# S5 products in fixed alternating rows, weights staged by half units, and the weights behind PLE ordered after the parts of x

## The chip, the cores and the metric

The kernel runs on one core of one Trainium2 chip. The metric is the device time of one execution in microseconds (us), the median of several runs. Nothing runs beside it on the chip's other cores.

## The reference

Two decoder layers over 256 tokens of width 1024, in float32. Each layer is `LN(a*x + 0.5*SwiGLU_1(x))`, then `LN(a*x + Mix(x))`, then `LN(a*x + 0.5*SwiGLU_2(x))`, then the gated embedding (PLE) `x + sigmoid(x Wg) * (p Wp)`. SwiGLU has an inner width of 2816. The mixer of layer 0 joins a Mamba-2 SSD (16 heads) and an S5 (64 groups of 16 channels, 64 complex states each); the mixer of layer 1 joins HGRN2 and GLA.

The S5 part matters here. Per group, `bu = B_bar u`, a diagonal complex recurrence `s[l] = lam_bar * s[l-1] + bu[l]`, and `y = Re(C s) + d * u`, followed by GELU and a gated projection. The kernel works on blocks of four time steps, so that there are 64 blocks in the sequence of 256: one product (`W`) folds a block's inputs into the states, a scan over the blocks carries them, one product (`Q`) reads the state before each block out, and one product (`T`) holds what a block's own inputs add to its outputs.

## The kernel before

**Weights.** All large weights lie in one array of units of 128 x 2048 float32 (1 MB). `Weights.unit` (L45) loads the next unit into a staging tile `wst` (two buffers of a whole unit), then splits each half `j` of it: ScalarE writes the rounded half `wh` (L61), VectorE writes the rest `wl` (L62). Every product with weights is three TensorE products (`wh` with `xh`, `wl` with `xh`, `wh` with `xl`). The split tiles have six buffers each, three units. The load is issued by SyncE, whose queue waits until VectorE has read the buffer's former contents.

**Order.** The program is written once, in Python, and a scheduler puts the instructions of each engine into an order of its own, by a simulated time line; buffers go round in program order. Each engine then runs its list strictly in that order on the chip. Two helpers bind the scheduler: `late` keeps an instruction where the program has it, and `behind(g, ins, anchors)` (L90) puts an instruction after named earlier ones of its own engine, as an order and not as a wait. `Weights.behind[n]` holds such anchors for unit `n`. `layer_norm` sets them for the units `at+1` and `at+2` of the next stage (last line of L117 to L145), `at` being the next unit to be loaded; `ple` sets none.

**Stages.** FFN 0 of layer 0 (`f00`), with the S5 parameters computed between its steps by `s5_scalars`, `s5_half` and `s5_params`; mixer AB; FFN 2 (`f01`); `ple_proj` and `ple` of layer 0; the same for layer 1 with mixer CD. An FFN has 11 steps of 256 inner columns: two units for gate and up (tile `gu_f`), one for down (tile `acc_f`). Its first step is `tile_major`: both units are loaded, and the products of token tile 0 come ahead of those of tile 1.

**S5 parameters.** For each of 8 batches of 8 groups, `s5_params(b)` computes tables on VectorE and returns `rest`, called a step later: 16 products of 64 x 64 (tile `s5w`, L543) turn two parts `i` of `E` round into two tiles `tp[0]`, `tp[1]` of the `tr` ring (two buffers in PSUM), which ScalarE copies out.

**S5 recurrence.** `s5_batches` (L661) is called four times in `ab_inputs`, for two batches `e = 0, 1` each, with the other projections of the mixer between the calls. It loads `W`, `tab`, `T` and `Q`; forms `v` of both batches (32 products of 64 x 64, L684) in the two buffers of the `mm` ring; and then, batch after batch on VectorE: `rotate`, two scans, `rotate` again into `S`. Then `y` of both batches (48 products, L712 for `T` and L715 for `Q`) in the `mm` ring again, and ScalarE copies `y` into `G`. A product takes 64 rows of the array, `row_half(0)` or `row_half(1)`. The program text lets `e = 0` and `e = 1` alternate, always in different halves, but nothing holds the scheduler to that. In the trace each of these float32 products is two MATMUL instructions.

**PLE.** `ple` forms `acc` for two halves `c` of the columns and two token tiles `t`; `finish(t, c)` takes tanh, combines, transposes the new `x` (tile `tp_ple`, L311) and splits it into `xh_ple`, `xl_ple` with `split_xT` (L112, L113). `split_xT` leaves its two instructions in `g.anchors`.

Of the kernel before, what the change touches and what calls it, by code (L numbers as in the profile page):

```python
# [17 lines left out]
P = 128  # L18
# [19 lines left out]
class Weights:  # L38
# [6 lines left out]
    def unit(self, pool=None):  # L45
        g, nc = self.g, self.g.nc
        pool = pool or g.wsp
        n = self.at
        self.at += 1
        st = g.wst.tile([P, 2048], F32, tag="wst", name=f"wst_{n}")  # L50
        step = {0: 512, 1: 1024, 2: 1024}.get(n, 2048)
        for c in (slice(i, i + step) for i in range(0, 2048, step)):
            nc.sync.dma_start(st[:, c], self.wall[n][:, c])
        out = []
        for j in range(2):
            wh = pool.tile([P, 1024], F32R, tag="wh", name=f"wh_{n}_{j}")
            wl = pool.tile([P, 1024], F32R, tag="wl", name=f"wl_{n}_{j}")
            src = st[:, j * 1024:(j + 1) * 1024]
            step = 512 if n == 0 else 1024
            for c in (slice(i, i + step) for i in range(0, 1024, step)):  # L60
                ops = [nc.scalar.copy(wh[:, c], src[:, c])]  # L61
                ops.append(nc.vector.tensor_tensor(wl[:, c], src[:, c], f32(wh[:, c]), op=ALU.subtract))  # L62
                for op in ops:
                    behind(g, op, self.behind.get(n, ()))
            out.append((wh, wl))
        return out
# [213 lines left out]
def ple(g, i, pp, out):  # L280

    nc = g.nc
    xT_in = g.xT
    last = out is not None
    acc = acc_tiles(g, f"ple{i}")
    units = [[None, None], [None, None]]
    xT = None if last else new_xT(g, f"ple{i}")
    xn = g.x

    def part(t, c, kh):  # L290
        for j in range(4):
            k = 4 * kh + j
            wh, wl = units[c][kh][j // 2]
            s = slice(512 * (j % 2), 512 * (j % 2) + 512)
            mm3(nc, acc[t][c], *of_tile(xT_in, t, k), wh[:, s], wl[:, s], k == 0, k == KT - 1)

    def finish(t, c):
        step = 256 if last and t == NT - 1 and c else 512
        for s in (slice(i, i + step) for i in range(512 * c, 512 * c + 512, step)):
            a = acc[t][c][:, s.start - 512 * c:s.stop - 512 * c]  # L300
            sg = g.pp.tile([P, step], F32, bufs=2, tag="ple_sg", name=f"sg_ple{i}_{t}_{s.start}")
            nc.scalar.activation(sg, a, AF.Tanh, scale=0.5)
            nc.vector.scalar_tensor_tensor(sg, sg, 1.0, pp[t][:, s], op0=ALU.add, op1=ALU.mult)
            nc.vector.scalar_tensor_tensor(xn[t][:, s], sg, 0.5, xn[t][:, s], op0=ALU.mult, op1=ALU.add)
            if last:
                nc.sync.dma_start(out[t * P:(t + 1) * P, s], xn[t][:, s])
        if last:
            return
        tp = g.ps.tile([P, 4, P], F32, tag="tr", name=f"tp_ple{i}_{t}_{c}", bufs=2)
        for k in range(4):  # L310
            nc.tensor.transpose(tp[:, k, :], xn[t][:, (4 * c + k) * P:(4 * c + k + 1) * P], g.ident)  # L311
        split_xT(g, t, c, tp, xT)

    for kh in range(2):
        units[0][kh] = g.w.unit()
    for t in range(NT):
        for kh in range(2):
            part(t, 0, kh)
    for t in range(NT):
        finish(t, 0)  # L320
    for kh in range(2):
        units[1][kh] = g.w.unit()
    for t in range(NT):
        for kh in range(2):
            part(t, 1, kh)
        finish(t, 1)
    g.xT = xT
# [172 lines left out]
def s5_params(g, b, half):  # L500
# [34 lines left out]
    def rest():  # L535
        W, K = g.s5pe
        Ev, Qv = (x.rearrange("p a (q n) -> p a q n", q=NP) for x in (E, Q))
        tp = [g.ps.tile([P, NP, 64], F32, tag="tr", name=f"s5w_{b}_{i}", bufs=2) for i in range(2)]
        for turn in range(2):
            for q in range(NP):  # L540
                for i in range(2):
                    r = row_half(turn ^ i)
                    nc.tensor.matmul(tp[i][r, q, :], Ev[r, i, q, :], g.ident[r, r], start=True, stop=True)  # L543
        for i in range(2):
            nc.scalar.copy(W[:, i], tp[i])
        kp = g.ps.tile([P, 64], F32, tag="tr", name=f"s5k_{b}", bufs=2)
# [87 lines left out]
    return ap.rearrange("p k (s c) -> p k s c", s=4)  # L634


def s5_inputs(g, pool, U, c):

    nc = g.nc
# [18 lines left out]
        nc.gpsimd.dma_start(to, dv[:, :, :, st, :])  # L658


def s5_batches(g, pool, U, G, bs):  # L661

    nc = g.nc
    mul, add, sub = ALU.mult, ALU.add, ALU.subtract
    W, T, Q, tab, S = [], [], [], [], []
    for b in bs:
        dram = g.s5dram[b]
        W.append(pool.tile([P, 2, NP, 64], F32, tag="W", name=f"W_{b}", bufs=3))  # L670
# [5 lines left out]
        Q.append(pool.tile([P, 2, NP, 80], F32, tag="Q", name=f"Q_{b}", bufs=3))  # L676
        nc.scalar.dma_start(Q[-1], dram[:, 1280:1920].rearrange("p (a q c) -> p a q c", a=2, q=NP))
    v = [g.ps.tile([P, 2, NP, 64], F32, tag="mm", name=f"s5v_{b}", bufs=2) for b in bs]
    for turn in range(2):
        for i in range(2):  # L680
            for q in range(NP):
                for e, b in enumerate(bs):
                    r = row_half(turn ^ e)
                    nc.tensor.matmul(v[e][r, i, q, :], W[e][r, i, q, :], U[r, NP * b + q, :], start=True, stop=True)  # L684

    for e, b in enumerate(bs):
        cosT, sinT, dec = (tab[e][:, 256 * i:256 * i + 256] for i in range(3))
        w = pool.tile([P, 2, 256], F32, tag="rw", name=f"rw_{b}", bufs=1)

        def rotate(src, name, out, ops):  # L690

            c = pool.tile([P, 2, 256], F32, tag="rotc", name=f"{name}c_{b}", bufs=2)
            s = pool.tile([P, 2, 256], F32, tag="rots", name=f"{name}s_{b}", bufs=2)
            nc.vector.tensor_tensor(c, src, bc(cosT, 1, 2), op=mul)
            nc.vector.tensor_tensor(s, src, bc(sinT, 1, 2), op=mul)
            for i in range(2):
                nc.vector.tensor_tensor(out[:, i], c[:, i], s[:, 1 - i], op=ops[i])

        m = pool.tile([P, 2, 256], F32, tag="rotm", name=f"rotm_{b}", bufs=1)
        rotate(v[e].rearrange("p a q c -> p a (q c)"), "rot", m, (add, sub))  # L700
        for i in range(2):
            nc.vector.tensor_tensor_scan(w[:, i], dec, m[:, i], 0.0, op0=mul, op1=add)
        S.append(pool.tile([P, 2, NP, 64], F32, tag="S", name=f"S_{b}", bufs=2))
        rotate(w, "rov", S[-1].rearrange("p a q c -> p a (q c)"), (sub, add))
    y = [g.ps.tile([P, NP, 64], F32, tag="mm", name=f"s5y_{b}", bufs=2) for b in bs]
    for turn in range(2):
        for q in range(NP):
            for i in range(-1, 2):
                for e, b in enumerate(bs):
                    r = row_half(turn ^ e)  # L710
                    if i < 0:
                        nc.tensor.matmul(y[e][r, q, :], T[e][r, q, :], U[r, NP * b + q, :], start=True,  # L712
                                         stop=False)
                    else:
                        nc.tensor.matmul(y[e][r, q, 1:64], Q[e][r, i, q, 16:80], S[e][r, i, q, 0:63],  # L715
                                         start=False, stop=i == 1)
    for e, b in enumerate(bs):
        lo = NP * b % 16
        nc.scalar.copy(G[:, lo:lo + NP, :], y[e])
# [252 lines left out]
def ab_inputs(g, pool, s5pool, yh, yl):  # L972
# [36 lines left out]
    U = s5pool.tile([P, 32, 64], F32, tag="U", name="U", bufs=1)  # L1009
    for c in range(2):  # L1010
        s5_inputs(g, pool, U, c)
    yT = []

    def recur(n):
        if n % 2 == 0:
            half.append(pool.tile([P, 16, 64], F32, tag="G", name=f"G_{n // 2}", bufs=1))
        s5_batches(g, s5pool, U, half[-1], (2 * n, 2 * n + 1))
        if n == 1:
            yT.append(s5_half_out(g, half[-1], 0, yh, yl))

# [278 lines left out]
def tile_trunk(ctx: ExitStack, tc: tile.TileContext, xnat, xTd, pT, lnr, colsd, cstd, abrow, abdt, s5bc, cdlr, cdgu,  # L1299
# [3 lines left out]
    g.nc, g.tc = nc, tc  # L1303
    g.abrow, g.abdt, g.s5bc, g.cdlr, g.cdgu = abrow, abdt, s5bc, cdlr, cdgu
    g.const = ctx.enter_context(tc.tile_pool(name="const", bufs=1))
    g.wst = ctx.enter_context(tc.tile_pool(name="wst", bufs=2))
    g.wsp = ctx.enter_context(tc.tile_pool(name="wsp", bufs=6))
    g.xp = ctx.enter_context(tc.tile_pool(name="xp", bufs=1))
    g.xt = ctx.enter_context(tc.tile_pool(name="xt", bufs=1))
# [225 lines left out]
```

## Time and profile before

| | |
|---|---|
| time, median of 3 runs | 1238.76 us (1238.2 to 1241.11) |
| the profiled execution | 1242.7 us, of which the span from the first to the last instruction is 1240.9 us |
| TensorE (PE) busy | 1210.4 us, 98% |
| weight loads into the array (PEld) | 1005.9 us, 81% |
| VectorE (DVE) busy | 854.5 us, 69% |
| ScalarE (ACT) busy | 583.9 us, 47% |
| GpSimd (POOL) busy | 72.4 us, 6% |
| DMA | 232.74 MB, 188 GB/s in the mean |
| granted TensorE clock | 0.993 in the mean |

Busy time is a union of modelled spans: matmuls are pipelined, so that a busy PE is not one at its peak, and successive starts tell what an instruction costs in a run. The profiled execution lies 3.9 us above the median of the three runs; the prediction works with differences from it.

### The profile page before, as it was taken

The numbers are of one execution on the slowest core, as the hardware profiler recorded it, in microseconds if no ns is written. First come the engines' busy times: TensorE is split into PE (matmuls) and PEld (weight loads), VectorE is DVE, ScalarE is ACT, GpSimd is POOL, SyncE is SP. The second block draws the span as 40 slices with busy tenths as digits, with TensorE's granted clock in tenths as the row PEclk, the third lists the DMA queues.
The fourth block names the chain that finished last, engine by engine and source line by source line (L and its number), as shares of the span: only waits on it lengthen the run. The fifth ranks groups of instructions, "written<-read, shape, count | busy, mean of one in ns | idle before, by whom it ended". The sixth has DMA issues, their size and how long they took to land.

```text
span 1240.9 us, 17250 instructions
## 1 busy us (share of the span) xinstructions
PE 1210.4 (98%) x6786; PEld 1005.9 (81%) x6786; DVE 854.5 (69%) x1352; ACT 583.9 (47%) x866; POOL 72.4 (6%) x124
## 2 busy tenths in 40 slices
PE   7999999999998999999998999999999999999998
PEld 6877777899887878888887888888888877888886
DVE  6999894688878766555567555456779776545466
ACT  5644452545535535443435444443674625444434
POOL 0012122110203000000000000000100010000000
PEclk9999999899999999999999999999999999999999
DMA  7567676775722647555536555554633327555532
GB/s 282 203 233 251 230 243 229 267 250 175 219 95 66 220 146 252 179 198 179 195 136 203 204 190 184 198 177 168 224 135 107 133 77 247 194 186 187 192 147 102
DMA packets 44609, 232.74 MB, mean 188 GB/s; under 512 B 9680, under 2 KB 10352, under 8 KB 20848
## 3 DMA queue, kind: packets, MB, share of 16 engines
q1 hardware_dynamic: 30672, 206.06, 48.2%
q0 software_dynamic: 4688, 14.16, 3.6%
q10 hardware_dynamic: 9168, 11.42, 2.8%
q8 instruction: 53, 0.87, 0.3%
q14 instruction: 28, 0.23, 0.1%
HBM read 219.56 MB, written 12.06 MB: 187 GB/s over the span
## 4 chain that ended last, share of the span: by engine, by line
PE 90%; DVE 4%; DMA 3%; ACT 2%; issue 1%; ACTq 0%; SPq 0%; DVEq 0%
PE gu_f L178 38%; PE acc_f L72 7%; PE acc_f L71 6%; PE acc_f L70 6%; DMA wst<-in_wall_dram 2%; PE pj_z L178 2%; PE ht_f L215 2%; DVE wl L62 2%; PE s5y L715 1%; PE acc_ab L72 1%; PE acc_ab L71 1%; PE acc_ab L70 1%; PE pj_u L178 1%; PE s5w L543 1%; PE pj_hg L178 1%; PE pj_gr L178 1%
## 5 line engine op out<-in xcount | busy, mean ns | idle before, releaser
L62 DVE TENSOR_TENSOR wl<-wst,wh 128x1024 fp32r<-128x1024 f32 (+1 forms) x378 | 453.1, 1216 | 259.3 <-ACT wh L61 251.5
L61 ACT CAST wh<-wst 128x1024 fp32r<-128x1024 f32 (+1 forms) x378 | 386.9, 1047 | 359.4 <-PE gu_f L178 109.0
L71 PE MATMUL acc_f<-wl,hh_f 128*128 128x512 f32 x352 | 137.9, 392 | 0.0
L70 PE MATMUL acc_f<-wh,hh_f 128*128 128x512 f32 x352 | 137.5, 390 | 0.0
L72 PE MATMUL acc_f<-wh,hl_f 128*128 128x512 f32 x352 | 135.9, 392 | 0.0
L72 PEld LDWEIGHTS acc_f<-wh,hl_f 128*128 128x128 f32 x352 | 66.1, 188 | 13.8
L71 PEld LDWEIGHTS acc_f<-wl,hh_f 128*128 128x128 f32 x352 | 66.1, 188 | 13.6
L70 PEld LDWEIGHTS acc_f<-wh,hh_f 128*128 128x128 f32 x352 | 66.1, 188 | 13.6
L178 PE MATMUL gu_f<-wh,xh_in 128*128 128x512 f32 x176 | 71.1, 409 | 5.9 <-ACT wh L61 5.9
L178 PE MATMUL gu_f<-wh,xh_ple 128*128 128x512 f32 x176 | 70.9, 403 | 3.5 <-ACT xh_ple L112 3.5
L178 PE MATMUL gu_f<-wh,xh_ab 128*128 128x512 f32 x176 | 69.8, 397 | 0.5 <-ACT xh_ab L112 0.5
L178 PE MATMUL gu_f<-wl,xh_ab 128*128 128x512 f32 x176 | 68.8, 391 | 1.3 <-DVE wl L62 1.3
L178 PE MATMUL gu_f<-wh,xh_cd 128*128 128x512 f32 x176 | 69.9, 397 | 0.0
L178 PE MATMUL gu_f<-wl,xh_in 128*128 128x512 f32 x176 | 69.8, 400 | 0.0
L178 PE MATMUL gu_f<-wl,xh_cd 128*128 128x512 f32 x176 | 68.8, 391 | 0.7 <-DVE wl L62 0.7
L178 PE MATMUL gu_f<-wl,xh_ple 128*128 128x512 f32 x176 | 69.5, 395 | 0.0
L211 ACT ACTIVATE sg_f<-gu_f 128x256 f32<-128x256 f32 x88 | 33.8, 384 | 70.4 <-PE gu_f L178 69.1
L178 PE MATMUL gu_f<-wh,xl_ab 128*128 128x512 f32 x176 | 66.9, 391 | 0.0
L178 PE MATMUL gu_f<-wh,xl_cd 128*128 128x512 f32 x176 | 66.8, 391 | 0.0
L178 PE MATMUL gu_f<-wh,xl_ple 128*128 128x512 f32 x176 | 66.7, 391 | 0.0
L178 PE MATMUL gu_f<-wh,xl_in 128*128 128x512 f32 x176 | 66.6, 392 | 0.0
L212 DVE TENSOR_TENSOR sg_f<-sg_f,gu_f 128x256 f32<-128x256 f32 x88 | 36.7, 417 | 27.2 <-ACT sg_f L211 27.0
(466 smaller groups left out, 2387.2 us busy)
## 6 DMA issues: line engine op xcount, KB each, us to landing
wst<-in_wall_dram SPq DMA_DIRECT2D x185, 1024.0 KB, 4.8
row<-in_lnr_dram SPq DMA_DIRECT2D x12, 512.0 KB, 6.7
s5d<-s5pk POOLq DMA_DIRECT2D x8, 704.0 KB, 5.1
tab<-s5d ACTq DMA_DIRECT2D x8, 384.0 KB, 3.5
Q<-s5d ACTq DMA_DIRECT2D x8, 320.0 KB, 4.2
wst<-in_wall_dram SPq DMA_DIRECT2D x4, 512.0 KB, 6.6
s5d<-s5W POOLq DMA_DIRECT2D x8, 256.0 KB, 4.6
W<-s5d ACTq DMA_DIRECT2D x8, 256.0 KB, 3.7
```

The source lines that it names most:

```text
L61: ops = [nc.scalar.copy(wh[:, c], src[:, c])]
L62: ops.append(nc.vector.tensor_tensor(wl[:, c], src[:, c], f32(wh[:, c]), op=ALU.subtract))
L70: nc.tensor.matmul(out, xh, wh, start=first, stop=False)
L71: nc.tensor.matmul(out, xh, wl, start=False, stop=False)
L72: nc.tensor.matmul(out, xl, wh, start=False, stop=last)
L178: nc.tensor.matmul(ps[t], x, w, start=kh == 0 and i == 0, stop=kh == 1 and i == len(mms) - 1)
L211: nc.scalar.activation(sg, ps[t][:, 0:256], AF.Silu)
L212: nc.vector.tensor_tensor(sg, sg, ps[t][:, 256:512], op=ALU.mult)
L215: nc.tensor.transpose(tp[:, k, :], sg[:, k * P:(k + 1) * P], g.ident)
L543: nc.tensor.matmul(tp[i][r, q, :], Ev[r, i, q, :], g.ident[r, r], start=True, stop=True)
L715: nc.tensor.matmul(y[e][r, q, 1:64], Q[e][r, i, q, 16:80], S[e][r, i, q, 0:63], start=False, stop=i == 1)
```

## The change

- `Weights.unit` stages half units: a tile of 128 x 1024, four buffers instead of two of twice the size; each half has a load of its own (512 KB, one instruction; four of 256 KB in all for unit 0, as before; units 1 and 2 were already loaded in two pieces). The splits are the same.
- `ple`: after the split of the second column half of tile `t`, `behind[at + 1 + t]` is set to the anchors, so that both engines' splits of the second unit behind PLE come after those of tile 0's second half, and those of the third unit after tile 1's.
- `in_row` puts each S5 product after the one before it on TensorE. In `rest` the 16 products keep the written order, alternating between row halves. In `s5_batches` both `v` and `y` keep a fixed order in which `e = 1` and `e = 0` alternate.
- In `y` the two `Q` products come first and `T` last, so that a group of products begins with one that needs `S` of batch 1. `S` holds the states shifted by one block, with a column of zeros put there once by GpSimd, so that `Q` products are 64 columns wide instead of 63; the last `rotate` writes 63 of 64 columns.

```diff
@@ Weights.unit
-        st = g.wst.tile([P, 2048], F32, tag="wst", name=f"wst_{n}")
-        step = {0: 512, 1: 1024, 2: 1024}.get(n, 2048)
-        for c in (slice(i, i + step) for i in range(0, 2048, step)):
-            nc.sync.dma_start(st[:, c], self.wall[n][:, c])
         out = []
         for j in range(2):
+            st = g.wst.tile([P, 1024], F32, tag="wst", name=f"wst_{n}_{j}")
...
             for c in (slice(i, i + step) for i in range(0, 1024, step)):
-                ops = [nc.scalar.copy(wh[:, c], src[:, c])]
-                ops.append(nc.vector.tensor_tensor(wl[:, c], src[:, c], f32(wh[:, c]), op=ALU.subtract))
+                nc.sync.dma_start(st[:, c], self.wall[n][:, 1024 * j + c.start:1024 * j + c.stop])
+            for c in (slice(i, i + step) for i in range(0, 1024, step)):
+                ops = [nc.scalar.copy(wh[:, c], st[:, c])]
+                ops.append(nc.vector.tensor_tensor(wl[:, c], st[:, c], f32(wh[:, c]), op=ALU.subtract))
@@ ple, finish
         split_xT(g, t, c, tp, xT)
+        if c:
+            g.w.behind[g.w.at + 1 + t] = g.anchors
@@ s5_params, rest
+        g.row = ()
         for turn in range(2):
             for q in range(NP):
                 for i in range(2):
                     r = row_half(turn ^ i)
-                    nc.tensor.matmul(tp[i][r, q, :], Ev[r, i, q, :], g.ident[r, r], start=True, stop=True)
+                    in_row(g, nc.tensor.matmul(tp[i][r, q, :], Ev[r, i, q, :], g.ident[r, r], start=True, stop=True))
@@ new
+def in_row(g, op):
+    behind(g, op, g.row)
+    g.row = (op.ins,)
@@ s5_batches, v
-                for e, b in enumerate(bs):
+                for e in (1, 0):
                     r = row_half(turn ^ e)
-                    nc.tensor.matmul(v[e][r, i, q, :], W[e][r, i, q, :], U[r, NP * b + q, :], start=True, stop=True)
+                    in_row(g, nc.tensor.matmul(v[e][r, i, q, :], W[e][r, i, q, :], U[r, NP * bs[e] + q, :], start=True,
+                                               stop=True))
@@ s5_batches, S and y
-        S.append(pool.tile([P, 2, NP, 64], F32, tag="S", name=f"S_{b}", bufs=2))
-        rotate(w, "rov", S[-1].rearrange("p a q c -> p a (q c)"), (sub, add))
+        rotate(w, "rov", S[e][:, :, :, 1:64], (sub, add), 63)
...
-            for i in range(-1, 2):
-                for e, b in enumerate(bs):
+            for i in range(3):
+                for e in (1, 0):
                     r = row_half(turn ^ e)
...
+                    k, x = (Q[e][r, i, q, 16:80], S[e][r, i, q, :]) if i < 2 else (T[e][r, q, :], U[r, NP * bs[e] + q, :])
+                    in_row(g, nc.tensor.matmul(y[e][r, q, :], k, x, start=i == 0, stop=i == 2))
@@ ab_inputs
+    S = [s5pool.tile([P, 2, NP, 64], F32, tag=f"S{e}", name=f"S{e}", bufs=1) for e in range(2)]
+    for e in range(2):
+        nc.gpsimd.memset(S[e][:, :, :, 0:1], 0.0)
@@ tile_trunk
-    g.wst = ctx.enter_context(tc.tile_pool(name="wst", bufs=2))
+    g.wst = ctx.enter_context(tc.tile_pool(name="wst", bufs=4))
```

## Rows read from the trace of the kernel before

**Rows 1.** The page, part 1: busy time, share, instructions by engine.
```profile
PE 1210.4 (98%) x6786; PEld 1005.9 (81%) x6786; DVE 854.5 (69%) x1352; ACT 583.9 (47%) x866; POOL 72.4 (6%) x124
```
**Rows 2.** The page, part 4: the chain that ended last, by engine.
```profile
PE 90%; DVE 4%; DMA 3%; ACT 2%; issue 1%; ACTq 0%; SPq 0%; DVEq 0%
```
**Rows 3.** Waits of PE, 250 to 368 us: total us, times, longest.
```profile
PE xs L996 <- ACT xsT L813: 0.2, 1, 0.2
```
**Rows 4.** Windows: start:end, length, busy by engine, PEclk, DMA share, GB/s.
```profile
20.00:216.00 196.00, 195.48 (x1173) 156.58 (x1172) 166.63 (x333) 95.43 (x161) 27.68 (x58) 1.00 0.66 231
...
250.00:360.00 110.00, 109.79 (x1108) 100.07 (x1107) 95.78 (x182) 52.19 (x71) 9.59 (x16) 1.00 0.63 197
360.00:400.00 40.00, 34.95 (x243) 28.02 (x241) 30.88 (x74) 19.48 (x44) 8.39 (x14) 0.96 0.17 41
```
**Rows 5.** Windows of tile `s5v` alone (PE, PEld, DVE): first two calls, sum.
```profile
250.00:262.00 12.00, 2.08 (x64) 1.94 (x64) 1.28 (x2) 1.00 0.85 263
...
280.00:300.00 20.00, 3.74 (x64) 3.52 (x64) 2.57 (x4) 1.00 0.56 177
...
sum 120.00, PE 14.14 PEld 12.79 DVE 10.27; mean PE 1.77 PEld 1.60 DVE 1.28
```
**Rows 6.** Windows of tile `s5y` alone (PE, PEld, DVE, ACT): one batch, sum.
```profile
300.00:310.00 10.00, 2.71 (x46) 2.58 (x46) 0.00 (x0) 0.38 (x1) 1.00 0.51 154
...
sum 120.00, PE 25.02 PEld 22.40 DVE 0.00 ACT 2.99; mean PE 3.13 PEld 2.80 DVE 0.00 ACT 0.37
```
**Rows 7.** Windows of tile `s5w` alone (PE, PEld, ACT): two stretches, sum.
```profile
60.00:75.00 15.00, 1.15 (x32) 1.01 (x32) 0.64 (x2) 1.00 0.59 210
...
115.00:130.00 15.00, 0.96 (x16) 0.82 (x16) 0.98 (x3) 1.00 0.81 265
...
sum 145.00, PE 14.44 PEld 12.25 ACT 5.53; mean PE 1.44 PEld 1.23 ACT 0.55
```
**Rows 8.** Timeline of PE: one `T` product among full-size products (start, us).
```profile
262.37 0.28 PE L581 MATMUL pc_bc<-xh_f,wl 128*128 128x256 f32 x1
262.57 0.32 PE L712 MATMUL s5y<-U,T 64*64 64x64 f32 x2
262.83 0.39 PE L579 MATMUL pc_bc<-xh_f,wh 128*128 128x256 f32 x1
```
**Rows 9.** Timeline, ends of first and fourth call: `S` of batch 1, then users.
```profile
276.80 0.75 DVE L697 TENSOR_TENSOR S<-rovc,rovs 128x256 f32<-128x256 f32 x2
...
281.25 0.32 PE L715 MATMUL s5y<-S,Q 64*64 64x63 f32 x2
...
359.71 0.76 DVE L697 TENSOR_TENSOR S<-rovc,rovs 128x256 f32<-128x256 f32 x2
...
367.02 1.43 DVE L853 TENSOR_TENSOR xd<-xs,dt 128x256 f32<-128x256 f32 x4 [2.08 <-PE s5y L715]
```
**Rows 10.** Timeline behind PLE, ACT then PE; in brackets the idle time before.
```profile
678.46 1.05 ACT L61 CAST wh<-wst 128x1024 fp32r<-128x1024 f32 x1 [3.13 <-DMA wst<-in_wall_dram]
679.42 1.06 ACT L112 CAST xh_ple<-tp_ple 128x512 fp32r<-128x512 f32 x2
...
672.80 1.03 PE L311 MATMUL tp_ple<-cs,x_ln 128*128 128x128 f32 x8
...
680.05 0.80 PE L178 MATMUL gu_f<-wh,xh_ple 128*128 128x512 f32 x1 [3.47 <-ACT xh_ple L112]
...
683.20 0.49 PE L178 MATMUL gu_f<-wl,xh_ple 128*128 128x512 f32 x1
```
**Rows 11.** Window behind PLE, columns as in group 4.
```profile
680.00:690.00 10.00, 9.95 (x41) 8.13 (x42) 6.54 (x9) 4.99 (x7) 0.00 (x0) 0.83 0.70 245
```
**Rows 12.** Windows at start-up and in a later FFN; DMA issues (count, KB, us).
```profile
10.00:20.00 10.00, 10.00 (x42) 7.92 (x41) 6.76 (x10) 5.01 (x6) 0.00 (x0) 1.00 0.97 371
...
720.00:850.00 130.00, 130.00 (x590) 107.56 (x589) 69.13 (x81) 59.31 (x80) 0.00 (x0) 1.00 0.56 194
...
wst<-in_wall_dram SPq DMA_DIRECT2D x4, 512.0 KB, 6.6
```

More of the change, by code (lines that the diff above doesn't have):

```diff
@@ L49, in unit @@
         self.at += 1
-        st = g.wst.tile([P, 2048], F32, tag="wst", name=f"wst_{n}")
-        step = {0: 512, 1: 1024, 2: 1024}.get(n, 2048)
-        for c in (slice(i, i + step) for i in range(0, 2048, step)):
-            nc.sync.dma_start(st[:, c], self.wall[n][:, c])
         out = []
         for j in range(2):
+            st = g.wst.tile([P, 1024], F32, tag="wst", name=f"wst_{n}_{j}")
             wh = pool.tile([P, 1024], F32R, tag="wh", name=f"wh_{n}_{j}")
             wl = pool.tile([P, 1024], F32R, tag="wl", name=f"wl_{n}_{j}")
-            src = st[:, j * 1024:(j + 1) * 1024]
             step = 512 if n == 0 else 1024
             for c in (slice(i, i + step) for i in range(0, 1024, step)):
-                ops = [nc.scalar.copy(wh[:, c], src[:, c])]
-                ops.append(nc.vector.tensor_tensor(wl[:, c], src[:, c], f32(wh[:, c]), op=ALU.subtract))
+                nc.sync.dma_start(st[:, c], self.wall[n][:, 1024 * j + c.start:1024 * j + c.stop])
+            for c in (slice(i, i + step) for i in range(0, 1024, step)):
+                ops = [nc.scalar.copy(wh[:, c], st[:, c])]
+                ops.append(nc.vector.tensor_tensor(wl[:, c], st[:, c], f32(wh[:, c]), op=ALU.subtract))
                 for op in ops:
@@ L658, in s5_inputs, with s5_batches @@
         nc.gpsimd.dma_start(to, dv[:, :, :, st, :])
-def s5_batches(g, pool, U, G, bs):
+def s5_batches(g, pool, U, G, S, bs):
     nc = g.nc
     mul, add, sub = ALU.mult, ALU.add, ALU.subtract
-    W, T, Q, tab, S = [], [], [], [], []
+    W, T, Q, tab = [], [], [], []
     for b in bs:
@@ L678, in s5_batches @@
     v = [g.ps.tile([P, 2, NP, 64], F32, tag="mm", name=f"s5v_{b}", bufs=2) for b in bs]
+    g.row = ()
     for turn in range(2):
@@ L688, in s5_batches, with rotate @@
         w = pool.tile([P, 2, 256], F32, tag="rw", name=f"rw_{b}", bufs=1)
-        def rotate(src, name, out, ops):
+        def rotate(src, name, out, ops, n=64):
             c = pool.tile([P, 2, 256], F32, tag="rotc", name=f"{name}c_{b}", bufs=2)
@@ L696, in rotate @@
             for i in range(2):
-                nc.vector.tensor_tensor(out[:, i], c[:, i], s[:, 1 - i], op=ops[i])
+                parts = (x.rearrange("p (q c) -> p q c", q=NP)[:, :, 0:n] for x in (c[:, i], s[:, 1 - i]))
+                nc.vector.tensor_tensor(out[:, i], *parts, op=ops[i])
         m = pool.tile([P, 2, 256], F32, tag="rotm", name=f"rotm_{b}", bufs=1)
-        rotate(v[e].rearrange("p a q c -> p a (q c)"), "rot", m, (add, sub))
+        rotate(v[e].rearrange("p a q c -> p a (q c)"), "rot", m.rearrange("p a (q c) -> p a q c", q=NP), (add, sub))
         for i in range(2):
             nc.vector.tensor_tensor_scan(w[:, i], dec, m[:, i], 0.0, op0=mul, op1=add)
-        S.append(pool.tile([P, 2, NP, 64], F32, tag="S", name=f"S_{b}", bufs=2))
-        rotate(w, "rov", S[-1].rearrange("p a q c -> p a (q c)"), (sub, add))
+        rotate(w, "rov", S[e][:, :, :, 1:64], (sub, add), 63)
     y = [g.ps.tile([P, NP, 64], F32, tag="mm", name=f"s5y_{b}", bufs=2) for b in bs]
+    g.row = ()
     for turn in range(2):
         for q in range(NP):
-            for i in range(-1, 2):
-                for e, b in enumerate(bs):
+            for i in range(3):
+                for e in (1, 0):
                     r = row_half(turn ^ e)
[L711 to L716, printed above, removed]
+                    k, x = (Q[e][r, i, q, 16:80], S[e][r, i, q, :]) if i < 2 else (T[e][r, q, :], U[r, NP * bs[e] + q, :])
+                    in_row(g, nc.tensor.matmul(y[e][r, q, :], k, x, start=i == 0, stop=i == 2))
     for e, b in enumerate(bs):
@@ L1016, in recur @@
             half.append(pool.tile([P, 16, 64], F32, tag="G", name=f"G_{n // 2}", bufs=1))
-        s5_batches(g, s5pool, U, half[-1], (2 * n, 2 * n + 1))
+        s5_batches(g, s5pool, U, half[-1], S, (2 * n, 2 * n + 1))
         if n == 1:
```

## The prediction

> **What bounds the kernel.** I read the page's busy times first. PE is busy 98% of the span and VectorE 69% [rows 1]; the chain that ended last is PE for 90% [rows 2]. A busy PE is not yet a full one, so the next view is the list of PE's waits: behind PLE PE waits 3.5 us [rows 10], and in the 118 us in which the S5 recurrence runs PE waits 0.2 us [rows 3]. So in those stretches PE runs its list without a gap, and time goes only where the list gets shorter, or until another engine is the bound. The windows say which engine that would be [rows 4]. In FFN 0, where the S5 parameters are made, VectorE is busy 166.6 of 196 us (85%). Where the recurrence runs, it is busy 95.8 of 110 us (87%), and behind it, from 360 to 400 us, 30.9 of 40 us while PE has gaps. In a later FFN it is busy 69.1 of 130 us [rows 12]. VectorE is therefore the next bound in the mixer, and nowhere else where the change shortens PE's list.
>
> **Part 1, S5 products in the mixer.** The first call's `v` ran as the program text alternates it: 64 instructions in 2.08 us, 32.5 ns each. The second call's 64 took 3.74 us, 58 ns each; all four calls took 14.14 us [rows 5]. One batch's `y` took 2.71 us for 46 instructions, 59 ns each, and all of `y` 25.02 us for 384 instructions [rows 6]. The reader is to see two speeds of one instruction. I read the slow one as products that follow one another in the same row half: the scheduler ran one batch by itself as soon as it was ready. After the change every product's neighbour is in the other half and in the other batch's PSUM tile, as in the fast call.
> PE's list shortens by: `v` 14.14 - 4 x 2.08 = 5.8 us; `y` 25.02 - 384 x 0.0325 = 25.02 - 12.5 = 12.5 us. Together 18.3 us. Lone `T` and `Q` products that the scheduler scattered between full-size ones go too: around one of them the next full-size product starts 0.46 us after the last instead of 0.12 [rows 8], but most of that is in the tile's own 25.02 us, and I add nothing.
>
> The two speeds above are two ways through the array. The Trainium skill, "TensorEngine Tiling (Array Packing)", sections "Tiling Modes" and "Gotcha 1", says that different tiles of the array load and multiply in parallel, that changing the mode drains the array, and that two row tiles must not meet in one PSUM bank. By that `y` would gain as `v` does, up to twofold, so 25.02 would fall to about 12.5, the same as by the rows.
>
> How much of the 18.3 us ends up in the time is VectorE's to say. Its recurrence work is not shortened. Upper bound: all 18.3 us. Lower bound: VectorE keeps its 87% share, and only the end of the fourth call gains. There `S` of batch 1 is ready at 359.71 + 0.76 = 360.5 us and the SSD heads, whose buffers lie where S5's lay, start at 367.0 us behind the last `y` [rows 9]. With both `y` in one run of 96 x 0.0325 = 3.1 us plus the 0.3 us to the heads, 6.5 us become 3.4: 3.1 us gained. I take a VectorE share of 93%, between 87% and full, since both batches' `y` and then both new `v` now lie between the end of one call's VectorE work and the next one's, and other splits and convolutions can only partly fill it: 95.8 / 0.93 = 103.0 instead of 110, so 7.0 us. With the 3.1 us at the end: 10 us (3 to 18).
>
> The fixed order has a price of its own: PE stands at the first `y` until batch 1 is through VectorE. In the trace the first lone product of batch 1 was reached 281.25 - 277.56 = 3.7 us after `S` was ready [rows 9], so this margin covers it. Work queued behind that product on PE would wait: the projections, and ScalarE and VectorE behind them.
> The zero column, the wider `Q` products (64 for 63) and the 63-column writes cost nothing that I can see: `T` products of 64 columns run in the same 59 ns train as those of 63 [rows 6].
>
> **Part 2, S5 products in the parameters.** `s5w` took 14.44 us for 256 instructions. Where 32 came as one alternating run it took 1.15 us, where 16 came alone 0.96 us [rows 7]. Eight alternating runs are 8 x 1.15 = 9.2 us: 5.2 us less. The run starts only when both `tr` buffers are free, so the first half runs some us later than now; `s5k` and the FFN's transposes come behind it in that ring, with a step of the FFN, 196 / 11 = 17.8 us, as cover. Bounds 0 and 5.2; PE has no wait in this stage and VectorE is at 85% [rows 4], so I take a value near the upper end: 4 us.
>
> **Part 3, the weights behind PLE.** PE stood 3.47 us before the first product of the next FFN. It waited for `xh_ple`; the transposes for it had started at 672.80 us, but ScalarE's list had a weight split ahead of it, and that waited 3.13 us for its load to land at 678.4 us [rows 10]. That split belongs to the second unit, which the change puts behind the parts of `x`. With it out of the way `xh_ple` of the first half can be ready before PE is done with `acc`, and the stall goes. The first seven starts after it are 3.15 us / 7 = 0.45 us apart [rows 10], against 130 / 590 = 0.22 in a later FFN [rows 12], and the granted clock of 680 to 690 us is 0.83 [rows 11]: after the idle time PE ran at the lower of its two levels, 1.2 instead of 2.4 GHz. Without the idle time 7 x 0.22 = 1.5 us go as well. Together 5.0 us at most. What is late next is the second unit: its splits come about 4 us earlier at PE's need and now behind `x` of tile 0, whose tanh, two VectorE steps and transpose lie in between. If they come late, PE waits there instead. Bounds: 5 us gained and 2 us lost (one more split of 1.05 us on ScalarE and its VectorE partner ahead of PE); I take 4.5 us gained, since the load had landed at 678.4 us, and PE would want it at about 682 us: it would begin at 680.05 - 3.47 = 676.6 us and has 24 products of the first unit to do, 5.4 us.
>
> **Part 4, half units.** The splits are as before; 185 loads of 1 MB become 370 of half the size, on a queue that issues nothing else of weight. A half buffer is free one VectorE split (about 1.2 us) sooner, so loads start earlier. Cover: in a later FFN the units need 194 GB/s at a DMA share of 0.56 [rows 12], which is 346 GB/s at a full share. At the start of the kernel, where loads came in pieces of 512 KB and less, DMA moved 371 GB/s at 0.97 [rows 12]; smaller pieces therefore don't lower the rate that can be had. I take 0, with 3 us either way, since the scheduler's lists will come out otherwise in every stage.
>
> The 512 KB loads of the start took 6.6 us to land [rows 12]; four in flight at that latency are 4 x 0.524 MB / 6.6 us = 318 GB/s, over the 194 needed. Against this stands a rule of the Trainium skill, "DMA: Bandwidth & Descriptors", section "Bandwidth": move at least 1 MiB per transfer for three quarters of the peak. Its fit, 2 us plus bytes over 436 GB/s, would give 3.2 us and, as an estimate, 164 GB/s for one half unit at a time, which is under the rate needed; with several in flight, as the rows show, it binds nothing.
>
> **Sum.** 10 + 4 + 4.5 + 0 = 18.5 us. The profiled execution's 1242.7 us become 1224.2. It lies 3.9 us above the median of the runs, so the median becomes 1238.8 - 18.5 = 1220 us.
>
> **Rivals.**
> R1, PE's whole saving is kept: 18.3 + 5.2 + 5.0 = 28.5 us, 1210 us. For it: no wait of PE in these stages. Against: 110 us less 15 would leave VectorE's 95.8 us no gap at all.
> R2, VectorE is the bound at once: 3.1 us at the end of the recurrence, 1 us of the parameters, 4.5 us behind PLE, together 8 to 9 us, 1230 us. For it: 87% is a mean, and its work comes in chains that PE feeds.
> R3, no gain: the scheduler puts the fixed runs where PE waits for them, and the waits eat the saving, within 3.7 us of 1238.8 us.
> R4, slower, by one mechanism: PE parks at `y`. Today batch 0's `y` is done while VectorE works on batch 1. If PE's list reaches the fixed run ahead of `S` of batch 1, all that stands behind it stops. A batch takes VectorE some 10 us, so up to 9 us per call, 36 us in all, less 18.3 + 8.5: 9 us slower, 1248 us. It decides from (18.3 + 8.5) / 4 = 6.7 us of parking per call. Against it: the lag of 3.7 us in today's list must be used up first [rows 9].
> The skill's rule on transfer size, if it held with several loads in flight, would be a fifth: 164 of 194 GB/s in the FFN stages. Four loads at 318 GB/s speak against it, and I give it 1%, with R4.
>
> **How the numbers follow.** Forecast (11 to 25 us faster) 0.55; R1 0.09; R2 (4 to 11 faster) 0.20; R3 0.08; R4 and the rule 0.08. About 0.3%, 3.7 us, is what a measurement tells from no change. Faster 0.84, same 0.08, slower 0.08. The range 1210 to 1237 us holds the forecast, R2, half of R1 and part of R3, some 0.82. The likeliest case's own range is 1214 to 1228.
>
> **What would show it.** Right: `s5v`, `s5y` and `s5w` at about 8, 13 and 9 us of PE; VectorE above 90% in the recurrence; no wait for `xh_ple` and no low clock behind PLE; FFN steps of unchanged length. Wrong: a PE wait on `S` at L715's successor, PE waits for `wl` in FFN 0 or behind PLE, FFN steps longer by a DMA wait, or 58 ns per product though they alternate.

## The result: 1252.6 us, 1.07% slower

The kernel after the change takes 1252.55 us (median; 1248.63 to 1255.9), the kernel before 1238.7 us beside it: a ratio of 1.0107, 95% interval 1.0074 to 1.0139. 1220 us were predicted, 1210 to 1237 as the range. The sign was wrong.

The page of the kernel after, busy times (against [rows 1]) and the chain that ended last (against [rows 2]):

```profile
PE 1196.2 (96%) x6786; PEld 991.9 (79%) x6786; DVE 857.8 (69%) x1352; ACT 585.5 (47%) x865; POOL 72.8 (6%) x126
...
PE 76%; DVE 5%; DMA 5%; issue 4%; ACT 2%; POOL 0%; ACTq 0%; SPq 0%; DVEq 0%; POOLq 0%
```

PE does less work than before (1196.2 against 1210.4 us) in a span of 1251.3 us instead of 1240.9. So its list did get cheaper and the time went into gaps: PE's share of the chain fell from 90% to 76%.

Windows of the kernel after on the S5 tiles alone: `s5v`, `s5y`, `s5w` (against [rows 5 to 7]):

```profile
250.00:400.00 150.00, 10.17 (x256) 9.52 (x256) 10.26 (x16) 0.91 0.56 165
```
```profile
250.00:400.00 150.00, 16.95 (x384) 16.36 (x384) 0.00 (x0) 2.56 (x8) 0.91 0.56 165
```
```profile
60.00:220.00 160.00, 11.41 (x256) 9.36 (x256) 5.13 (x16) 0.99 0.67 229
```

The products gained 4.0, 8.1 and 3.0 us. What they gained is less than what PE lost waiting. PE's waits in the kernel after (total us, times, longest); the first two lines lie in the recurrence, where [rows 3] has 0.2 us in all, the last two in FFN 0, where the kernel before waits for neither `hh_f` nor `s5K`:

```profile
PE s5y L722 <- issue: 17.2, 2, 10.4
...
PE s5v L692 <- DMA U<-udram: 2.7, 1, 2.7
...
PE acc_f L68 <- ACT hh_f L216: 2.1, 4, 0.7
...
PE ht_f L213 <- ACT s5K L554: 1.6, 1, 1.6
```

Windows of the kernel after (PE, PEld, DVE, ACT, POOL, then granted clock, DMA share, GB/s); the first is FFN 0, the second the recurrence from the first `v` to the last `y` (against [rows 4]), the next two its second half, the last a `y` run behind a wait:

```profile
20.00:204.00 184.00, 180.63 (x1067) 142.72 (x1066) 158.60 (x316) 90.02 (x150) 22.47 (x48) 0.99 0.70 236
266.00:382.00 116.00, 96.68 (x1123) 90.38 (x1123) 91.29 (x177) 47.22 (x65) 9.60 (x16) 0.88 0.56 169
...
340.00:360.00 20.00, 9.59 (x141) 8.58 (x137) 17.05 (x30) 6.22 (x8) 5.69 (x11) 0.70 0.78 211
360.00:380.00 20.00, 13.19 (x202) 12.69 (x200) 10.28 (x20) 0.65 (x2) 0.00 (x0) 0.76 0.09 25
...
356.00:361.00 5.00, 5.00 (x95) 4.90 (x92) 1.29 (x2) 1.14 (x2) 0.00 (x0) 0.50 0.50 169
```

The third and fourth calls of the recurrence, timeline of PE in the kernel after:

```profile
339.10 2.08 PE L692 MATMUL s5v<-U,W 64*64 64x64 f32 x64
...
344.83 0.39 PE L176 MATMUL pj_z<-wh,xl_f 128*128 128x512 f32 x1
...
355.63 0.76 PE L722 MATMUL s5y<-S,Q 64*64 64x64 f32 x8 [10.41 <-issue]
...
363.97 2.08 PE L692 MATMUL s5v<-U,W 64*64 64x64 f32 x64
...
376.29 0.77 PE L722 MATMUL s5y<-S,Q 64*64 64x64 f32 x8 [6.81 <-issue]
```

and VectorE in the same stretch:

```profile
342.64 0.68 DVE L703 TENSOR_TENSOR rotc<-s5v,tab 128x512 f32<-128x512 f32 x1
...
355.11 0.75 DVE L707 TENSOR_TENSOR S<-rovc,rovs 128x252 f32<-128x252 f32 x2
...
366.11 0.69 DVE L703 TENSOR_TENSOR rotc<-s5v,tab 128x512 f32<-128x512 f32 x1 [6.51 <-PE s5v L692]
...
375.77 0.75 DVE L707 TENSOR_TENSOR S<-rovc,rovs 128x252 f32<-128x252 f32 x2
...
381.83 1.43 DVE L859 TENSOR_TENSOR xd<-xs,dt 128x256 f32<-128x256 f32 x4 [5.31 <-PE s5y L722]
```

Read the two together. PE reaches the tied `y` at 345.2 us and stands until VectorE writes `S` of batch 1, from 355.11 us on; then VectorE stands until the tied `v` is through, then PE again, then VectorE again. Each engine waits for the other in turn. After either wait PE runs at the lower of its two clock levels, 1.2 GHz: from 356 to 361 us the granted clock is 0.50 (in the two longer windows it is 0.70 and 0.76 in the mean), and the 96 instructions of `y` that take 3.0 us in the first call (290.88 to 293.89 us) take 5.5 us here (355.63 to 361.09 us). In the kernel before, `xd` came at 367.02 us [rows 9]: 14.8 us later now, of which 9.6 us had been lost before the first `v` (256.5 to 266.2 us), in FFN 0 and behind it, and 5.2 us within the recurrence. So there are two losses to explain, and the larger one lies ahead of the recurrence.

### The profile page after: what moved, and what is told of

It is laid out like the page before. It is cut to its first block, busy times and chain, and to the rows that moved or that the text cites. A ratio compares the mean times of both kernels' runs of the same rounds, so it can differ in the third digit from the quotient of the medians.

```text
span 1251.3 us, 17862 instructions
## 1 busy us (share of the span) xinstructions
PE 1196.2 (96%) x6786; PEld 991.9 (79%) x6786; DVE 857.8 (69%) x1352; ACT 585.5 (47%) x865; POOL 72.8 (6%) x126
## 4 chain that ended last, share of the span: by engine, by line
PE 76%; DVE 5%; DMA 5%; issue 4%; ACT 2%; POOL 0%; ACTq 0%; SPq 0%; DVEq 0%; POOLq 0%
PE gu_f L176 30%; PE acc_f L68 6%; PE acc_f L70 6%; PE acc_f L69 6%; DMA wst<-in_wall_dram 3%; PE pj_z L176 2%; PE ht_f L213 1%; PE acc_ple L69 1%; PE acc_ab L70 1%; PE acc_ab L68 1%; PE acc_ab L69 1%; PE acc_ple L68 1%; PE acc_ple L70 1%; DVE wl L60 1%; PE s5y L722 1%
## 5 line engine op out<-in xcount | busy, mean ns | idle before, releaser
L68 PEld LDWEIGHTS acc_f<-wh,hh_f 128*128 128x128 f32 x352 | 66.0, 188 | 17.3 <-ACT hh_f L216 4.0
L69 PEld LDWEIGHTS acc_f<-wl,hh_f 128*128 128x128 f32 x352 | 66.0, 188 | 13.6
## 6 DMA issues: line engine op xcount, KB each, us to landing
s5d<-s5W POOLq DMA_DIRECT2D x8, 256.0 KB, 4.7
W<-s5d ACTq DMA_DIRECT2D x8, 256.0 KB, 3.8
wst<-in_wall_dram SPq DMA_DIRECT2D x4, 256.0 KB, 5.9
```

What stands on the lines that cost most here:

```text
L68: nc.tensor.matmul(out, xh, wh, start=first, stop=False)
L69: nc.tensor.matmul(out, xh, wl, start=False, stop=False)
```

## The experiments

Theory at the outset: the loss is PE parked at `y`. Rivals: the half units' loads, and the fixed `s5w` in FFN 0. As the parts came in, two theories stood against each other: A, the cost comes from *tying* two PSUM tiles into one run, so that the run, and all that follows from it, waits for the later one; B, any fixed run costs, because it holds up what stands behind it. All ratios are to the kernel before on the same chip, with their 95% intervals.

**The parts alone, or together.** Each is the kernel before with these hunks of the diff and no others:

```
e1   Weights.unit and the wst pool (half units)
e2   ple: g.w.behind[g.w.at + 1 + t] = g.anchors
e5   in_row, rest                    (s5w)
e6   in_row, v                       (s5v)
e7   in_row, y, shifted S            (s5y)
e3   e5 + e6 + e7     e4   all but e7      e8   all but e5      e12  e1 + e5
```

> Only the staging in half units. Two theories for the 14 us lost: parking (PE stands 17 us at the fixed y runs, and that is all of it) and staging (FFN 0 and the start of mixer AB became 10 us longer, with waits for half-unit loads). Parking: no change beyond 4 us, 1235 to 1242 us. Staging: 1245 us or more, with the first v product of the S5 recurrence near 266 us instead of 256.5.

Measured: 1239.38 us, 1.0015 (0.9993 to 1.0037). No effect that can be told from none, as part 4's term of 0 had it.

> Only the order of the weights behind PLE. Both theories: the wait for xh_ple and the low clock behind it go, 4 to 5 us faster, 1234 us; no change elsewhere.

Measured: 1240.14 us, 1.0011 (0.9995 to 1.0027). No gain; both theories had expected one, and missed.

> Only the S5 products in fixed rows, all three kinds. Parking: 5 to 12 us slower, 1244 to 1251 us, with PE waits of 10 us or more at a y run. Staging: faster by 5 to 10 us, 1229 to 1234 us, without such waits, since nothing then delays the recurrence.

Measured: 1247.93 us, 1.0084 (1.0053 to 1.0115), with one wait of 9.6 us at `y`. The S5 runs alone are slower.

> The whole change but for y, which stays in the free order of before, T first. Parking: the waits go, and s5w, v and PLE keep their gains: 1225 to 1233 us. Staging: the 10 us of FFN 0 and the start of the mixer stay, 1240 us or more.

Measured: 1253.46 us, 1.0126 (1.0101 to 1.0151). This felled the theory at the outset: without the fixed `y` the kernel is as slow as with it. Parking at `y` is not the cause, or not the only one.

> Only the s5w products of FFN 0 in a fixed alternating order; staging, PLE and the mixer as before. Theory A (the fixed order makes FFN 0 longer, since the run needs both tr buffers and s5k and the transposes of the FFN stand behind it): s5w near 11 us of PE, the last gu_f of FFN 0 at 198 to 204 us instead of 195.8, PE waits for hh_f or s5K of 2 us or more, and 1241 to 1247 us. Theory B (FFN 0 is not the cause, the mixer is): last gu_f within 1.5 us of 195.8 and 1236 to 1240 us.

Measured: 1241.65 us, 1.0020 (1.0004 to 1.0035); last `gu_f` of FFN 0 at 200.3 us.

> Only the s5v products in a fixed alternating order; the list of PE is that of before up to the first s5v. Theory A (FFN 0 carries the loss): s5v from 14.1 to 8 to 10 us, first s5v at 256.5 us as before, 1234 to 1239 us. Theory B (a fixed run in the mixer is held up: it waits for both mm buffers and for W and U of both batches, and what stands behind it on PE waits with it): waits of PE before s5v of 2 us or more, last s5v later than 348.8 us by 3 to 10 us, 1241 to 1248 us.

Measured: 1245.27 us, 1.0057 (1.0041 to 1.0073), although `s5v` fell from 14.1 to 9.5 us; `s5y`, which was left free, rose from 25.0 to 29.1 us. PE does not wait at `v`, as theory B had it, but 5.2 us at the `y` behind it. This is the dearest of the five parts, and the one the prediction had not suspected. Timeline of PE in e6, first the products of the third call's `v`, then the last of `y` of the second call's batch 1:

```profile
309.79 0.32 PE L691 MATMUL s5v<-U,W 64*64 64x64 f32 x2
320.43 0.91 PE L691 MATMUL s5v<-U,W 64*64 64x64 f32 x22
```
```profile
316.80 0.39 PE L723 MATMUL s5y<-S,Q 64*64 64x63 f32 x4
```

and ScalarE and VectorE in e6:

```profile
317.42 0.37 ACT L727 COPY G<-s5y 128x256 f32<-128x256 f32 x1 [2.18 <-PE s5y L723]
```
```profile
323.22 1.23 DVE L62 TENSOR_TENSOR wl<-wst,wh 128x1024 fp32r<-128x1024 f32 x1 [6.34 <-ACT wh L61]
...
325.81 0.68 DVE L702 TENSOR_TENSOR rotc<-s5v,tab 128x512 f32<-128x512 f32 x1
```

The run is seen torn in two, in PE's list itself, since PE has other work in between: one product (two MATMUL instructions) goes into the free `mm` buffer at 309.79 us; the next one wants the other buffer, which holds `y` of batch 1 until the copy at 317.42 us; the rest of the run comes at 320.43 us. A buffer that could have fed VectorE lies open and unused for 10.6 us, and VectorE stands idle for 6.3 us before it has work again. In the kernel before, `v` of one batch went in from 311.54 us on, among the products of the other buffer's `y`.

> Only the s5y products in a fixed alternating order, with the shifted S; v, s5w, staging and PLE as before. Theory A (FFN 0 carries the loss): s5y from 25.0 to 13 to 17 us, waits of PE before s5y under 4 us in all, 1230 to 1239 us. Theory B (PE stands at the first product of a fixed y until S of the second batch is ready): waits before s5y of 8 us or more in all, calls three and four above all, y then at the lower clock, 1242 to 1250 us.

Measured: 1239.6 us, 1.0010 (0.9992 to 1.0027). PE waited 12.5 us in all at `y`, longest 6.8, and the time is that of before: here the wait and the saving cancel. That is the wait of theory B, with a time between the ranges of A and B.

> The whole change without the fixed order of s5w in FFN 0. Theory A: the loss of the whole change is mostly that of FFN 0, so last gu_f near 196 us, first s5v near 257 us, and 1236 to 1242 us. Theory B: FFN 0 as before, but PE still stands at s5y for 12 to 17 us in all, and 1246 to 1252 us.

Measured: 1248.37 us, 1.0086 (1.0067 to 1.0105); first `v` at 259.2 us, waits at `y` 10.6 us. So with `s5w` free most of the loss is still there; the next run shows that FFN 0 can lose as much without the mixer. The five parts alone add up to 0.15 + 0.11 + 0.20 + 0.57 + 0.10 = 1.13%, the whole measured 1.07%; that the two agree is chance, since not all the parts add.

> Half-unit staging and the fixed s5w rows together, mixer and PLE as before. Alone they moved the start of S5 by +1.2 and +3.2 us, in the whole change it is +9.6 us. Theory A (the two hurt each other in FFN 0): last gu_f of FFN 0 at 201 to 204 us, first s5v at 264 to 267 us, 1245 to 1249 us. Theory B (they only add, the rest comes from the other parts): last gu_f at 199 to 201 us, first s5v near 261 us, 1241 to 1244 us.

Measured: 1248.73 us, 1.0082 (1.0051 to 1.0113); last `gu_f` at 202.6 us, first `v` at 264.4 us. These two parts do not add: alone 0.15% and 0.20%, together 0.82%. With the mixer as before this is nearly the loss of e8, which has the mixer's runs: each of the two losses is there without the other.

**The runs untied.** The same fixed runs, but each within one batch (or one parameter tile): its two row halves alternate in its own PSUM tile, and no product waits for another tile.

```diff
 # e9: y. e11: v too. e13: s5w too. e15: e13 + e2. e14: e13 + e1 + e2.
-    for turn in range(2):
-        for q in range(NP):
-            for i in range(3):
-                for e in (1, 0):
-                    r = row_half(turn ^ e)
+    for e in range(2):
+        g.row = ()
+        for q in range(NP):
+            for i in range(3):
+                for r in (row_half(0), row_half(1)):
 ...
 # e16: as e9, with "for r" as the outermost of the three loops
 # e10: as e9, with one mm tile for each half, y[j][r, q, :], and two copies to G
```

> s5y of each batch in a fixed order of its own: the two row halves of one batch alternate in that batch's one PSUM tile, so no product waits for the other batch; T comes last, S is shifted; v, s5w, staging and PLE as before. Theory A (tying two batches together is what costs: the next v and the VectorE work behind it start later): calls of the recurrence some 27 to 30 us apart as before, last glu at 405 to 411 us (411.9 before). If the halves overlap in one bank s5y falls to 13 to 16 us and the time to 1229 to 1236 us; if they do not, s5y stays near 23 to 25 us and the time near 1239 us. Theory B (any fixed run costs, tied or not): 1242 us or more.

Measured: 1227.3 us, 0.9904 (0.9874 to 0.9934). Last `glu` at 398.1 us; before, 411.9. Both lie below theory A's ranges: the calls came sooner than it had them.

> As e9, but the two row halves of a batch write two PSUM tiles, in different banks, so y of a batch needs both mm buffers. s5y then at 13 to 15 us. Theory A (what counts is how soon the next v and y may start): y of the second batch and the next v wait for one more buffer, so calls are 28 to 31 us apart and the time lies between e9 with overlap and e7, 1234 to 1241 us. Theory B (any fixed run costs): 1242 us or more.

Measured: 1232.0 us, 0.9941 (0.9922 to 0.9959), between e9 and e7 as theory A has it, but below its range. With two buffers for a batch PE waits 4.3 us at `y`, of them 1.1 us for the copies to `G`.

> e9 with the two row halves of a batch one after the other instead of alternating: one run for each batch, T last, S shifted, but neighbours in the same half. If alternating is what makes a product 33 ns instead of 59: s5y at 22 to 25 us and 1234 to 1239 us. If it is the unbroken run: s5y at 13 to 16 us and 1227 to 1230 us.

Measured: 1236.97 us, 0.9983 (0.9968 to 0.9998). Windows of tile `s5y` over the four calls, e9 and then e16 (25.02 us before [rows 6]):

```profile
250.00:400.00 150.00, 13.13 (x384) 11.93 (x384) 0.00 (x0) 2.95 (x8) 0.99 0.57 182
```
```profile
250.00:400.00 150.00, 23.36 (x384) 21.71 (x384) 0.00 (x0) 2.97 (x8) 0.99 0.52 164
```

So it is the alternation that nearly halves the price of an instruction (13.13 us / 384 = 34 ns against 61 ns), not the unbroken run, and two halves in one tile do it as well as two halves in two.

> e9 with v of each batch in a fixed order of its own too, halves alternating in one tile. Theory A: first VectorE step of each call no later than before, time at or below that of e9 by 0 to 4 us. Theory B: v in a fixed order costs about what it cost in e6, so some 5 to 7 us above e9.

Measured: 1224.86 us, 0.9892 (0.9854 to 0.9930). `v` in a fixed order costs nothing when it is not tied, where tied it had cost 0.57%.

> e11 with s5w in a fixed order of its own as well: the row halves of one parameter tile alternate in that one tr tile, so a run needs one tr buffer and not both. Theory A (the tied run for both tr buffers is what cost 2.5 us in e5): s5w at 10 to 12 us, last gu_f of FFN 0 at 193 to 197 us, no wait for s5K or hh_f over 1 us, 1221 to 1226 us. Theory B (products in one run hold back s5k and the transposes of the FFN, tied or not): last gu_f at 199 us or later, 1226 to 1229 us.

Measured: 1222.42 us, 0.9872 (0.9845 to 0.9898), the fastest kernel of the study beside e15; last `gu_f` at 194.1 us, `s5w` 11.11 us of PE. Theory A holds in FFN 0 too, by the time of the last `gu_f` (196.3 us in e11); the times of e11 and e13 are too near each other to tell.

> e13 with the splits behind PLE, without half units. If the wait behind PLE is a steady cost, 3 to 5 us below e13; if it is an accident of the profiled execution of before (in six other profiles it is 1.2 to 2.1 us long), within 2 us of e13.

Measured: 1222.58 us, 0.9872 (0.9856 to 0.9889). The same as e13.

> The whole change with its three fixed runs untied: half-unit staging, the splits behind PLE, and s5w, s5v, s5y each in the order of one batch (or one parameter tile). Theory A (tying is the one cause of the loss, the half units only add to it through the tied s5w): first s5v at 255 to 260 us, last glu at 396 to 402 us, 1218 to 1227 us. Theory B (the half units cost time by themselves where S5's loads and theirs meet): first s5v at 262 us or later, 1230 to 1238 us.

Measured: 1226.02 us, 0.9903 (0.9885 to 0.9921); first `v` at 256.0, last `glu` at 398.8 us. Nothing but the order of the three runs differs from the kernel after. The whole change with its runs untied is 0.97% faster where the change itself is 1.07% slower. Tying the runs, in the order that they have here, is the cause.

Tied and untied mixers differ in the time from the first VectorE step of the first call to that of the fourth, worked out from the first `rotc` of each call:

```
                       first call   fourth   apart    time
e13  own w, v, y          254.98    332.80    77.8   1222.4
e14  the whole, own       257.22    337.77    80.6   1226.0
e11  own v, y             257.24    337.91    80.7   1224.9
e9   own y                258.73    340.43    81.7   1227.3
e12  half units, tied w   267.97    352.75    84.8   1248.7
before                    258.97    344.02    85.1   1239
e16  own y, no altern.    259.13    346.62    87.5   1237.0
e10  own y, two tiles     259.14    346.75    87.6   1232.0
e7   tied y               260.30    352.61    92.3   1239.6
after                     269.84    366.11    96.3   1252.6
e3   tied w, v, y         261.27    358.79    97.5   1247.9
e4   the whole but y      269.26    366.77    97.5   1253.5
e6   tied v               257.62    356.12    98.5   1245.3
e8   the whole but s5w    261.42    360.52    99.1   1248.4
```

Untied and alternating within one tile 78 to 82 us, before 85, tied 92 to 99; the kernel after and e4 have a late first call on top, and in e12 the late first call is nearly the whole loss. This time does not order the kernels by itself: e10 lies above the kernel before and is faster. What goes with the time in all 18 kernels is the last `glu`, the end of the mixer of layer 0: from 393.0 us in e13 to 426.9 in e4. From there to the end every profiled execution takes 823 to 831 us, so most of what these kernels differ by lies ahead of it. Here it is before and then after (first and last start in us):

```profile
L760 PE MATMUL glu<-yh,wl x64: 279/283/283, 354.4 to 411.9; 128*128 128x256 f32 x64
```
```profile
L766 PE MATMUL glu<-yh,wl x64: 278/283/283, 361.6 to 425.4; 128*128 128x256 f32 x64
```

Timeline rows of VectorE behind the lines of e6 and e13:

```profile
257.62 0.68 DVE L702 TENSOR_TENSOR rotc<-s5v,tab 128x512 f32<-128x512 f32 x1
...
356.12 0.69 DVE L702 TENSOR_TENSOR rotc<-s5v,tab 128x512 f32<-128x512 f32 x1 [1.27 <-PE s5v L691]
```
```profile
254.98 0.68 DVE L701 TENSOR_TENSOR rotc<-s5v,tab 128x512 f32<-128x512 f32 x1
...
332.80 0.68 DVE L701 TENSOR_TENSOR rotc<-s5v,tab 128x512 f32<-128x512 f32 x1
```

and a window of e13 over the recurrence, in the columns of [rows 4]: VectorE at 95%, PE at 99%.

```profile
250.00:350.00 100.00, 98.77 (x1169) 90.18 (x1167) 95.18 (x188) 52.06 (x73) 9.59 (x16) 1.00 0.66 214
```

## Why the prediction was wrong, step by step

**The steps that failed** are two, and they weigh about the same. Part 1 had 10 us gained in the recurrence; 5.2 us were lost there. Part 2 had 4 us gained ahead of it and part 4 nothing lost; the first `v` comes 9.6 us later.

**Part 1, the recurrence.** What failed is "I take a VectorE share of 93%", together with "this margin covers it". The share was read as what the new list would reach if VectorE were kept fed, and the price of the fixed order as one margin of the old list, 3.7 us at one call. Neither asks what the tie does to the cycle of the calls. That cycle is `S` of batch 1, `y`, copy, next `v`, first VectorE step. In the kernel before, from `S` ready to the next first step it took 8.7, 9.7 and 7.8 us at the three changes of call; in the kernel after 14.0, 14.7 and 10.3 us; in e6 13.6, 15.0 and 11.6 us. The three times of before could have been read off its trace, and the path that the tie adds (both copies, then both `v`, in the place of one) too. VectorE's share fell from 87% to 91.29 / 116 = 79%. The prediction's own first sign of being wrong, a PE wait on `S` at the successor of L715, is what the page shows: 17.2 us at L722. The estimate of 93% itself was right for a list without the tie: e13 shows 95%.

**The margin.** At the first call of the kernel after, `y` starts 0.05 us after `S` of batch 1 is written (290.88 against 290.08 + 0.75 us); the 3.7 us of [rows 9] were used up at once. The margin was a property of the old list, not of the work.

**R4** named the right place and sign, but its mechanism is half of it: PE parked 10.4 and 6.8 us in two of the four calls, 4.3 us a call in the mean, which is less than the 6.7 us from which it was to decide, and e4 is slow without any fixed `y`. That its time (1248 us) is near the measured one is luck: it set 36 us of parking against 26.8 us of gains; what came was half the parking, none of the gain in time, and the cost of the tied `v` and `s5w`, which R4 did not have.

**Speed of the products**: right. 32 to 34 ns an instruction when neighbours alternate, as in the fast call of [rows 5]; e16 shows that it is the alternation.

**Part 2, the parameters**, is the second step that failed: `s5w` fell by 3.0 us (5.2 hoped for), and the sentence that named the danger ("the first half runs some us later than now") gave it a step of the FFN as cover, which did not cover it. The fixed `s5w` alone moves the first `v` from 256.5 to 259.7 us (e5), with half units to 264.4 us (e12); the whole change has 266.2. Timeline of PE in the kernel after, one step of FFN 0:

```profile
185.75 0.44 PE L213 MATMUL ht_f<-cs,sg_f 128*128 128x128 f32 x2 [1.63 <-ACT s5K L554]
...
186.57 0.33 PE L544 MATMUL s5w<-cs,s5e 64*64 64x64 f32 x2
...
196.86 1.14 PE L544 MATMUL s5w<-cs,s5e 64*64 64x64 f32 x30
...
203.07 0.44 PE L213 MATMUL ht_f<-cs,sg_f 128*128 128x128 f32 x2
```

The run is torn as `v` in e6 is: one product opens it, the rest follows 10 us later, and the transposes of the FFN, which use the same ring, come 17.3 us after the last ones; before, 182.50 to 195.10 us, 12.6. PE stood 1.6 us, and from 180 to 200 us the granted clock was 0.91 in the mean. With the run untied (e13) the first `v` comes 2.9 us earlier than before: of the forecast's 4 us that much was there to be had.

**Part 3, behind PLE**: the wait for `xh_ple` went as foreseen (3.5 to 0.5 us), but nothing came of it in e2 or e15. The 3.5 us were one execution's: in nine other profiles of kernels that stage and order their weights as before, it was 1.2 to 2.1 us, as here in e5 and e9:

```profile
PE gu_f L178 <- ACT xh_ple L112: 1.2, 1, 1.2
```
```profile
PE gu_f L178 <- ACT xh_ple L112: 2.1, 1, 2.1
```

In [rows 10] the wait ends with a load's landing; that this is what differs from execution to execution is likely, but was not followed up. The execution from which the term was read is itself 3.9 us above the median. The size of the term was wrong, 4.5 us for something near nothing.

**Part 4, half units**: 0 was right for e1 by itself, but they have a price at one place: `s5v` waits 2.0 to 3.2 us for `U` in every kernel that has them (e1, e4, e8, e12, e14, after), and in none without. DMA issues of the kernel after and of e13 (count, KB each, median us from issue to landing):

```profile
udram<-uT POOLq DMA_DIRECT2D x2, 512.0 KB, 6.7
```
```profile
udram<-uT POOLq DMA_DIRECT2D x2, 512.0 KB, 4.8
```

The first of the two stores of `U`, which the loads of `U` wait for, lands 6.2 to 8.0 us after its issue in these six kernels and 3.1 to 3.3 us in the twelve others; the loads behind it land somewhat sooner (in the median 4.2 to 4.7 us against 5.1 to 7.3). Four pieces of weights instead of two may be in flight beside the store; that this is why was not tested. e14, which has half units and the order behind PLE, is 3.6 us above e13, which has neither, at the edge of what these runs can tell. Against the rule of the Trainium skill, "DMA: Bandwidth & Descriptors", section "Bandwidth", which asks for 1 MiB per transfer (its table is of transfers that GpSimd issued; the weights' loads are SyncE's), the bulk loads themselves lost nothing that shows: the interval of e1's ratio includes 1. What part 4 did not ask is what half units do beside the tied `s5w`: e12 is 0.82% slower, e5 0.20%.

**What stays open**: why half units and tied `s5w` together (e12) cost 0.82% when the sum of the two is 0.35%. The first `v` of e12 comes 4.7 us behind that of e5: 2.3 us are there at the last `gu_f` of FFN 0 (202.6 against 200.3 us), 2.6 us are the wait for `U`. Why FFN 0 ends later, though half units alone end it a little sooner (195.0 us in e1, 195.8 before), was not traced. Not tried either is a tied run in another order: the tied runs of the mixer begin with batch 1, and `y` with a product that needs its `S`, so the price of the tie and that of this order are one number here. That the scheduler's lists differ in every variant is part of each of these numbers.

## What to carry to other kernels

An order that interleaves two independent chains for the sake of a cheaper instruction ties their buffers and their readiness together; before it is costed by the cheaper instruction, the cycle from one chain's result to the next use of its buffer has to be written down and lengthened by the wait for the later of the two. Look first for the same gain inside one chain: here the two row halves of one batch alternate as well as two batches do, and give 1.28% (e13; 0.97% with the change's other parts, e14) where the tie lost 1.07%. A run that begins as soon as its first buffer is free holds that buffer until the last one is, and the trace shows it as one or two instructions far ahead of the rest.

## What the runs showed of the hardware

Products of 64 x 64 in the two row halves, alternating and writing the same PSUM tile, follow one another every 34 ns (13.13 us for 384 instructions in e9), much as when the halves write two different tiles (x64 in 2.08 us, 32.5 ns [rows 5]); neighbours in the same half take 61 ns (e16). I had expected that the halves would have to be in different banks, as the Trainium skill, "TensorEngine Tiling (Array Packing)", section "Gotcha 1", states; no run here shows a cost of one tile for both. In these products each half writes 64 partitions of its own; halves that write the same partitions were not tried.
